# Paired dilated heads, weights of a later stage split and stored ahead, convolution taps in small groups

## The chip, the cores and the metric

The kernel runs on one core of one Trainium2 chip. The metric is the device time of one execution in microseconds. Three runs of the kernel before took 2578.41, 2578.83 and 2579.85 us, so its median is 2578.83 us.

## The reference, cut to what matters

A sequence of 512 positions with 1024 channels, in float32, goes through two blocks of two layers each.

```python
# first block, each of two layers
p = rms_norm(x, norm_g[layer]) @ w_in[layer]
a = mla_attention(...) * silu(gate_a)
b = dilated_attention(dil_qkv, cos_d, sin_d) * silu(gate_b)   # 8 heads of 64, three groups
x = x + concatenate([a, b], -1) @ w_out[layer]

# dilated attention: in each group a banded softmax attention over keys at stride 1, 4 or 16,
# then the three outputs are mixed by softmax of their log-sum-exp

# second block, layer l in (0, 1)
shift, scale, gate = split(silu(c) @ ada_w[l, s] + ada_b[l, s], 3)
h = rmsnorm(x) * (1 + scale) + shift
# l = 0: a gated recurrence (hgrn) and an rwkv mixer
# l = 1: the mixer in question
p = h @ cd_w_in                                    # 1024 x 1536
y_c = real(fftn(p[:, :512], over positions and each 128 channels))
y_d = silu(layernorm(dwconv31(val * sigmoid(gate_))))   # val, gate_ = split(p[:, 512:], 2)
x = x + gate * (concatenate([y_c, y_d], -1) @ cd_w_out)
# after each mixer, the feed forward
u, v = split(h @ w_up, 2)                          # 1024 x 5632
x = x + gate * ((silu(dwconv3(u)) * v) @ w_down)   # 2816 x 1024
```

## The kernel before

Channels lie on the 128 partitions and the 512 positions on the free axis, so x is 8 tiles of 128x512. A float32 product is made of three passes of the reduced format f32r: each operand is split into a high part and a remainder, and TensorE adds high by high, high by low and low by high (`mm3`, L130 to L132). A gemm (`gemm`) makes one 128x512 output tile from a slab of weights of 128x1024 floats (512 KB): SyncE loads the slab into `wraw`, ScalarE copies it to `whi` (L75), VectorE subtracts to `wlo` (L76), and TensorE runs 24 matmuls. The tiles `wraw`, `whi` and `wlo` have three buffers each, so a slab can be loaded three gemms ahead.

The order on each engine is not that of the code: a scheduler lays the instructions of all stages into one program for each engine. Every engine then takes its own instructions strictly in that order, SyncE its DMAs too: one that waits holds up all behind it.

Stages that matter here, by their place in the trace:

- Dilated attention, 267 to 497 us in the first layer and 820 to 1013 us in the second. `operands(p)` makes queries and keys of two heads, with rotary factors (L590 to L602; the multiply of L591 is GpSimd's). `attention(p)` handles two heads e = 0, 1, one after the other: scores `sc` (L620 to L623), maximum and exponential (L627 to L632), factors `fa` by which the three groups are weighted (L649 to L657), a multiply of the probabilities by them (L663, VectorE), transposes on TensorE into `tp` (L669, L671), copies to `pt` (L674 to L678, ScalarE), and products with the values into `po` (L683, L688). A head fills 64 of the 128 rows of `po`. There are four calls in a layer. Gemms of the next p stand in between.
- First feed forward, about 1626 to 1996 us: two halves, each of 22 gemms up and 8 gemms down. In the first half 48 slabs of modulation weights (`adaw`, 512 KB each, two buffers) are loaded for later layers and multiplied on VectorE (L719). Padded tiles `padt` are cleared at both edges by GpSimd (L750) and filled by ScalarE (L751).
- The mixer of the second block's layer 1, `m3`, 1996 to 2190 us: `conformer_in`, `fourier`, `conformer_conv` with 31 taps for each of four tiles (L1447, L1449 on VectorE; 23 taps of the last tile on TensorE through diagonal matrices `cdg` that GpSimd builds, L1439), `conformer_norm`, and `out_proj` twice. Its 24 slabs (12 of `cd_w_in`, 4 of the Fourier matrix `dft_s`, 8 of `cd_w_out`, the last as 16 halves) go the usual way through `wraw`.

Of the kernel before, what the change touches and what calls it, by code (L numbers as in the profile page):

```python
# [12 lines left out]
ALU = mybir.AluOpType  # L13
# [11 lines left out]
class Ctx:  # L25
# [165 lines left out]
    def out_proj_steps(self, pool, W, k0, mix, xcol, gate=None, done=None, norm=None, parts=None):  # L191
# [9 lines left out]
        late = 0 if norm is None else norm.late if n == 8 else 3  # L201
        for o in range(KD - late):
            xc = xcol(o)
            ps = self.gemm(W[:, o, k0:k0 + n], mh, ml, n)
            self.add_x(xc, ps, gate, o)
            if done is not None:
                done(o, xc)
            if norm is not None:
                norm.tile(o)
            yield  # L210
        if norm is not None and not late:
            norm.finish()
        if late:
            last = range(KD - late, KD)
            ws = [self.wslab(W[:, o, k0:k0 + n], [128, n, 128]) for o in last]
# [18 lines left out]
def at(x, k):  # L234

    return x[k] if isinstance(x, list) else x[:, k, :]

# [178 lines left out]
def block1_mixers(c, l, nm, mixf, side, w0, fill):  # L416
# [4 lines left out]
    if True:  # L421
# [114 lines left out]
        with ExitStack() as e2:  # L536
# [42 lines left out]
            def operands(p):  # L579
# [5 lines left out]
                for gi in range(3):  # L585
                    for j in range(2):
# [4 lines left out]
                        nc.gpsimd.tensor_tensor(sh, sh, roped[:, 1, :], op=ALU.mult)  # L591
# [15 lines left out]
            def attention(p):  # L607
                q0, k0, k0l, qk12 = qk.pop(p)
                po = c.pz.tile([128, S], F32, name="po", tag="pz")
                for e in range(2):  # L610
                    eb = slice(64 * e, 64 * e + 64)
                    hcol = slice(128 * p + 64 * e, 128 * p + 64 * e + 64)
                    st = dp.tile([128, 2, 2, 4], F32, name="st", tag="st", bufs=2)
                    nm = dp.tile([128, 2, 4], F32, name="nm", tag="nm", bufs=2)
                    pp = dp.tile([128, 4, S], F32, name="pp", tag="pp", bufs=2)
                    for i in range(4):
                        w0 = (0, 64, 192, 256)[i]
                        sc = c.px.tile([128, S], F32, name="sc", tag="px")
                        tq = slice(128 * i, 128 * i + 128)
                        nc.tensor.matmul(sc[:, 0:256], lhsT=q0[:, e, tq], rhs=k0[:, e, w0:w0 + 256], start=True, stop=False)  # L620
                        nc.tensor.matmul(sc[:, 0:256], lhsT=q0[eb, e, tq], rhs=k0l[eb, w0:w0 + 256], start=False, stop=True)
                        for gi in range(2):
                            nc.tensor.matmul(sc[:, 256 + 128 * gi:384 + 128 * gi], lhsT=qk12[eb, 0, gi, tq],  # L623
                                             rhs=qk12[eb, 1, gi, tq], start=True, stop=True)
                        for z in range(2):
                            w = slice(256 * z, 256 * z + 256)
                            nc.vector.tensor_tensor_reduce(pp[:, i, w], in0=sc[:, w], in1=dmask[:, 4 * z or i, :], scale=1.0, scalar=3 * NEG,  # L627
                                                           op0=ALU.add, op1=ALU.max, accum_out=st[:, 0, z, i:i + 1])
                        nc.vector.tensor_scalar(nm[:, :, i], st[:, 0, :, i], -0.125, None, op0=ALU.mult)  # L629
                        for z in range(2):  # L630
                            pz = pp[:, i, 256 * z:256 * z + 256]
                            nc.scalar.activation(pz, pz, AF.Exp, bias=nm[:, z, i:i + 1], scale=0.125,  # L632
                                                 accum_out=st[:, 1, z, i:i + 1])

                    ex = dp.tile([128, 2, 2, 128], F32, name="ex", tag="ex", bufs=2)
                    bc = lambda t: t.rearrange("p (z o n) -> p z o n", z=1, o=1).to_broadcast([128, 2, 4, 32])
                    nc.vector.tensor_tensor(ex[:, 0].rearrange("p z (i n) -> p z i n", i=4),
                                            st[:, :, 0, :].rearrange("p z (i o) -> p z i o", o=1).to_broadcast([128, 2, 4, 32]),
                                            bc(sel[:, 0:32]), op=ALU.mult)
                    nc.vector.tensor_tensor(ex[:, 1].rearrange("p z (n r) -> p z r n", r=4),  # L640
                                            st[:, :, 1, :].rearrange("p z (i o) -> p z i o", o=1).to_broadcast([128, 2, 4, 32]),
# [7 lines left out]
                    nc.vector.tensor_tensor(M, st[:, 0], ot[:, 0], op=ALU.max)  # L649
                    nc.vector.tensor_tensor(e1, st[:, 0], M, op=ALU.subtract)  # L650
                    nc.vector.tensor_tensor(e2_, ot[:, 0], M, op=ALU.subtract)
                    nc.scalar.activation(fa[:, 1:3], fa[:, 1:3], AF.Exp, scale=0.125)
                    nc.vector.tensor_tensor(f, e1, st[:, 1], op=ALU.mult)
# [3 lines left out]
                    nc.vector.tensor_tensor(f, f, e1, op=ALU.mult)  # L657

                    pts = []
                    for i in range(4):  # L660
                        for z in range(2):
                            pz = pp[:, i, 256 * z:256 * z + 256]
                            nc.vector.tensor_scalar(pz, pz, f[:, z, i:i + 1], None, op0=ALU.mult)  # L663

                        blocks = (((0, 0, 64, 0), (64, 0, 128, 1)), ((0, 0, 128, 1), (128, 0, 128, 2)),
                                  ((0, 0, 128, 2), (128, 0, 128, 3)), ((192, 64, 64, 0), (64, 0, 128, 3)))[i]
                        tp = c.py.tile([128, 4, 128], F32, name="tp", tag="py")
                        for j, (o, r0, n, vt) in enumerate(blocks):
                            nc.tensor.transpose(tp[0:n, j, :], pp[:, i, o:o + n], c.ident)  # L669
                        for j in range(2):  # L670
                            nc.tensor.transpose(tp[:, 2 + j, :], pp[:, i, 256 + 128 * j:384 + 128 * j], c.ident)  # L671
                        pt = dp.tile([128, 4, 128], F32, name="pt", tag="pt", bufs=4)
                        if i in (1, 2):
                            nc.scalar.activation(pt, tp, AF.Copy)  # L674
                        else:
                            r0 = blocks[0][1]
                            nc.scalar.activation(pt[r0:r0 + 64, 0, :], tp[0:64, 0, :], AF.Copy)
                            nc.scalar.activation(pt[:, 1:4, :], tp[:, 1:4, :], AF.Copy)  # L678
                        pts.append((pt, blocks))
                    for i in range(4):  # L680
                        pt, blocks = pts[i]
                        for j, (o, r0, n, vt) in enumerate(blocks):
                            nc.tensor.matmul(po[eb, 128 * i:128 * i + 128], lhsT=v0[r0:r0 + n, vt, hcol],  # L683
                                             rhs=pt[r0:r0 + n, j, :], start=i == 0 and j == 0, stop=False)
                    for i in range(4):
                        pt, _ = pts[i]
                        for j in range(2):
                            nc.tensor.matmul(po[eb, i::4], lhsT=v12[:, j, i, hcol], rhs=pt[:, 2 + j, :],  # L688
# [1353 lines left out]
```

## Time and profile before

| | |
|---|---|
| median of three runs | 2578.83 us |
| the profiled execution, device time | 2578.49 us |
| its span in the trace | 2576.7 us |
| mean granted TensorE clock | 0.976 of full speed |
| TensorE busy | 2488.2 us, 97% of the span |
| VectorE busy | 1643.1 us, 64% |
| ScalarE busy | 1074.9 us, 42% |
| GpSimd busy | 220.6 us, 9% |

The busy time of TensorE counts a matmul as running while its columns stream, and matmuls overlap by their pipelines, so intervals are read from start to start in the timeline. All DMAs of the program go through SyncE's queue (and two small queues for instructions). The share of the DMA engines is a mean over 16 engines.

### The profile page before, as it was taken

The page shows a single profiled execution, that of the slowest core. Times are in us where ns is not written, and L with a number is a line of the kernel's source. Part 1 is how long each engine was busy: PE and PEld are TensorE (multiplying, and loading weights), DVE is VectorE, ACT ScalarE, POOL GpSimd, SP SyncE. Part 2 cuts the span into 40 slices and gives each one's busy share as a digit, 9 for nine tenths or more (in the row PEclk, how much of TensorE's full clock was granted, in tenths as well). Part 3 has the DMA queues.
Part 4 walks back from the last instruction along what each step waited for, and adds up shares of the span by engine and source line. Part 5 has one row for each costly group of instructions (what it writes and reads, how often), then busy time and mean ns, then how long its engine had stood idle before and what let it go on. Part 6 is the DMA issues. An engine that isn't in the chain of part 4 may idle for free. (4 is left out here: it accounts for less than half of the span.)

```text
span 2576.7 us, 38952 instructions
## 1 busy us (share of the span) xinstructions
PE 2488.2 (97%) x15261; PEld 1999.1 (78%) x15261; DVE 1643.1 (64%) x3261; ACT 1074.9 (42%) x1947; POOL 220.6 (9%) x303
## 2 busy tenths in 40 slices
PE   8999999999999999999999888999999989999998
PEld 6769777787697777877677777878888767888887
DVE  5767666647677666576576575786444797543544
ACT  5653333526534335555434652532333424432331
POOL 0000111000001110211000130200000210100000
PEclk9999999999999999999999978999999989999999
DMA  4137121331271213321211422586333403233322
GB/s 150 45 127 241 54 58 56 109 111 40 93 278 58 58 58 95 105 74 51 88 48 55 143 81 82 190 269 209 101 88 122 149 1 97 80 88 103 96 83 81
DMA packets 92023, 265.09 MB, mean 103 GB/s; under 512 B 14528, under 2 KB 27072, under 8 KB 90944
## 3 DMA queue, kind: packets, MB, share of 16 engines
q1 hardware_dynamic: 91840, 262.61, 32.5%
q8 instruction: 120, 1.97, 0.3%
q14 instruction: 63, 0.52, 0.1%
HBM read 246.06 MB, written 16.52 MB: 102 GB/s over the span
## 5 line engine op out<-in xcount | busy, mean ns | idle before, releaser
L75 ACT ACTIVATE whi<-wraw 128x1024 fp32r<-128x1024 f32 (+3 forms) x370 | 348.5, 943 | 774.6 <-PE pg L131 563.7
L130 PE MATMUL pg<-hh,whi 128*128 128x512 f32 x1560 | 629.3, 403 | 7.9 <-ACT whi L124 6.6
L131 PE MATMUL pg<-hl,whi 128*128 128x512 f32 x1560 | 630.9, 404 | 0.0
L132 PE MATMUL pg<-hh,wlo 128*128 128x512 f32 x1560 | 628.0, 403 | 0.0
L76 DVE TENSOR_TENSOR wlo<-wraw,whi 128x1024 fp32r<-128x1024 f32 (+4 forms) x366 | 422.6, 1156 | 284.8 <-ACT whi L75 281.2
L130 PEld LDWEIGHTS pg<-hh,whi 128*128 128x128 f32 x1560 | 295.8, 190 | 88.0 <-ACT whi L124 6.6
L131 PEld LDWEIGHTS pg<-hl,whi 128*128 128x128 f32 x1560 | 295.8, 190 | 76.7 <-issue 8.1
L132 PEld LDWEIGHTS pg<-hh,wlo 128*128 128x128 f32 x1560 | 296.2, 190 | 71.6 <-issue 2.5
L132 PE MATMUL pg<-hidh,wlo 128*128 128x512 f32 (+1 forms) x396 | 145.5, 367 | 0.3 <-DVE wlo L76 0.3
L131 PE MATMUL pg<-hidl,whi 128*128 128x512 f32 (+1 forms) x396 | 145.6, 368 | 0.0
L130 PE MATMUL pg<-hidh,whi 128*128 128x512 f32 (+1 forms) x396 | 145.1, 366 | 0.0
L719 DVE CUSTOM_DVE_ANT_0 adaw<-adaw,sc 128x1024 f32<-128x1024 f32 x96 | 116.3, 1225 | 41.0 <-DMA adaw<-in_ada_w_dram 33.4
L591 POOL TENSOR_TENSOR shf<-shf,roped 128x512 f32<-128x512 f32 x48 | 62.0, 1292 | 532.7 <-ACT whi L75 249.2
L130 PE MATMUL pgv<-whi,hh 128*128 128x512 f32 (+1 forms) x240 | 89.7, 374 | 0.0
L132 PE MATMUL pgv<-whi,hl 128*128 128x512 f32 (+1 forms) x240 | 88.4, 368 | 0.0
L131 PE MATMUL pgv<-wlo,hh 128*128 128x512 f32 (+1 forms) x240 | 88.3, 368 | 0.0
L632 ACT ACTIVATE pp<-pp,nm 128x256 f32<-128x256 f32 x128 | 63.6, 497 | 54.9 <-DVE nm L629 54.8
L130 PEld LDWEIGHTS pg<-hidh,whi 128*128 128x128 f32 x396 | 74.3, 188 | 13.6 <-issue 0.4
L132 PEld LDWEIGHTS pg<-hidh,wlo 128*128 128x128 f32 x396 | 74.4, 188 | 13.1 <-DVE wlo L76 1.0
L131 PEld LDWEIGHTS pg<-hidl,whi 128*128 128x128 f32 x396 | 74.4, 188 | 12.7
L1529 ACT ACTIVATE fu<-fu 128x512 f32<-128x512 f32 x44 | 27.8, 631 | 112.2 <-DVE fu L745 112.2
L231 DVE SCALAR_TENSOR_TENSOR xT<-pg,mod,xT 128x512 f32<-128x512 f32 (+1 forms) x54 | 38.2, 710 | 48.5 <-PE pg L132 48.4
(512 smaller groups left out, 4486.2 us busy)
## 6 DMA issues: line engine op xcount, KB each, us to landing
adaw<-in_ada_w_dram SPq DMA_DIRECT2D x96, 512.0 KB, 4.6
wraw<-in_ffn_up_dram SPq DMA_DIRECT2D x88, 512.0 KB, 3.6
wraw<-in_w_dqk_dram SPq DMA_DIRECT2D x48, 512.0 KB, 3.6
wraw<-in_ffn_down_dram SPq DMA_DIRECT2D x32, 512.0 KB, 3.6
wraw<-in_w_dv_dram SPq DMA_DIRECT2D x24, 512.0 KB, 3.7
wraw<-in_w_gate_dram SPq DMA_DIRECT2D x16, 512.0 KB, 3.7
wraw<-in_w_out_dram SPq DMA_DIRECT2D x16, 512.0 KB, 3.7
wraw<-in_w_hg_dram SPq DMA_DIRECT2D x16, 512.0 KB, 3.7
```

The costliest lines, as they stand in the source:

```text
L75: nc.scalar.activation(hi, raw, AF.Copy)
L76: (eng or nc.vector).tensor_tensor(lo, raw, hi.bitcast(F32), op=ALU.subtract)
L130: mm(out, lhsT=ah, rhs=bh, start=first, stop=False)
L131: mm(out, lhsT=ah, rhs=bl, start=False, stop=False)
L132: mm(out, lhsT=al, rhs=bh, start=False, stop=last)
L231: self.nc.vector.scalar_tensor_tensor(x, in0=ps, scalar=gate[:, o:o + 1], in1=x, op0=ALU.mult, op1=ALU.add)
L591: nc.gpsimd.tensor_tensor(sh, sh, roped[:, 1, :], op=ALU.mult)
L632: nc.scalar.activation(pz, pz, AF.Exp, bias=nm[:, z, i:i + 1], scale=0.125, accum_out=st[:, 1, z, i:i + 1])
L719: nc.vector.tensor_tensor_reduce(w, in0=w, in1=sc, scale=1.0, scalar=0.0, op0=ALU.mult, op1=ALU.add, accum_out=mod[:, j:j + 1])
L1529: nc.scalar.activation(u, u, AF.Silu)
```

## The change

**Dilated heads.** The two heads of a call go together: the score matmuls, the copies and the `po` matmuls are written in turns of e = 0 and e = 1, so that neighbours use different halves of TensorE's rows or columns. VectorE's multiply L663 is gone. In its place ScalarE builds, for every head and block of 128 queries, two diagonal matrices `dg` of 128x128 with the factors (L705 of the changed kernel), and the transposes become fp32 matmuls of the probabilities against `dg` (L709, L711). `pt` reuses the memory of `pp`, with a clearing by GpSimd for the edge blocks. The rotary multiply L591 moves from GpSimd to VectorE.

**Weights ahead.** A class `Parts` takes each of the 24 slabs of `m3`: inside the first feed forward it loads the slab (`praw`, two buffers, SyncE), splits it (`phi` on ScalarE, `plo` on VectorE, two buffers each) and writes both parts to DRAM, 512 KB each, by DMAs of GpSimd's queue. In `m3` a gemm loads the two parts straight into `whi` and `wlo` and splits nothing.

**Taps.** `conformer_conv` becomes a class `Conv`, whose `taps(n)` is called between the gemms of `conformer_in` and `fourier`; the diagonal matrices, TensorE's taps and what is left follow in `rest`, after the first step of the first half of `out_proj`.

```diff
     def wslab(self, src, shape, raw=None, eng=None, out=None):
+        if isinstance(src, Parts):
+            hl = out or [self.w.tile(shape, F32R, name=t, tag=t) for t in ("whi", "wlo")]
+            for t, z in zip(hl, src.parts):
+                nc.sync.dma_start(t.bitcast(F32), z)
+            return hl
...
+class Parts:
+    def __init__(self, c, src, name):
+        self.src = src.rearrange("p k n -> p (k n)")
+        self.parts = [c.dram.tile([128, 1024], F32, name=f"{name}{z}") for z in "hl"]
+    def make(self, c, pool):
+        raw = pool.tile([128, 1024], F32, name="praw", tag="praw", bufs=2)
+        c.nc.sync.dma_start(raw, self.src)
+        hl = [pool.tile([128, 1024], F32R, name=t, tag=t, bufs=2) for t in ("phi", "plo")]
+        c.split(*hl, raw)
+        for z, t in zip(self.parts, hl):
+            c.nc.gpsimd.dma_start(z, t.bitcast(F32))
...
-                        nc.gpsimd.tensor_tensor(sh, sh, roped[:, 1, :], op=ALU.mult)
+                        nc.vector.tensor_tensor(sh, sh, roped[:, 1, :], op=ALU.mult)
...
-                            nc.vector.tensor_scalar(pz, pz, f[:, z, i:i + 1], None, op0=ALU.mult)
+                            nc.scalar.activation(dg[:, z], c.ident, AF.Copy, scale=fs[e][:, z, i:i + 1])
...
-                            nc.tensor.transpose(tp[0:n, j, :], pp[:, i, o:o + n], c.ident)
+                            mm(tp[0:n, j, :], lhsT=pp[e, i][:, o:o + n], rhs=dg[:, 0], start=True, stop=True)
...
+                for i in range(4):
+                    for j in range(2):
+                        for e, eb, hcol in es:
+                            pt, blocks = pts[e, i]
+                            nc.tensor.matmul(po[eb, 128 * i:128 * i + 128], lhsT=v0[:, blocks[j][3], hcol], rhs=pt[:, j, :],
+                                             start=i == 0 and j == 0, stop=False)
...
+    def taps(self, n):
+        nc, cw, acc = self.c.nc, self.cw, self.acc
+        while n and self.todo and self.todo[0][0] < len(self.hds):
+            j, t = self.todo.pop(0)
...
             ps = c.gemm(I["ffn_up"][l][:, 2 * j], hh, hl)
             p = padded(c, fp, ps)
+            if ahead is not None:
+                ahead()
...
         for o in range(KD - late):
             c.side()
+            if ahead is not None and not hf:
+                ahead()
...
-                cv = conformer_in(c, dp, hh, hl)
-                fourier(c, dp, hh, hl, mixf)
+                cv = Conv(c, dp)
+                conformer_in(c, dp, hh, hl, cv)
+                fourier(c, dp, hh, hl, mixf, cv)
                 x = load_x(Norm, *spec)
-                acc = conformer_conv(c, dp, hp, cv)
-                conformer_norm(c, dp, acc, mixf)
-                c.out_proj(mp, W, 0, [mixf[:, k] for k in range(4)], x, gate)
+                half = c.out_proj_steps(mp, W, 0, [mixf[:, k] for k in range(4)], x, gate)
+                next(half)
+                cv.rest(dp, hp)
+                conformer_norm(c, dp, cv.acc, mixf)
+                for _ in half:
+                    pass
...
+                todo = [c.parts["in"][k] for k in (8, 4, 9, 5, 10, 6, 11, 7, 0, 1, 2, 3)] + c.parts["dft"] + c.parts["out"]
+                ahead = lambda: todo and todo.pop(0).make(c, fp)
```

Where the scheduler puts things shows in the programs of the engines. A row there gives the line, the instruction, its output and inputs with tile numbers, and the shape.

On TensorE, at the end of the first layer's first attention call, the kernel before runs the `po` matmuls of one head in a row:

```order
L671 MATMUL tp_2311<-c_ident_81,pp_2222 128x128 x2
L683 MATMUL po_2219<-pt_2288,v0_1512 64x128
L683 MATMUL po_2219<-pt_2298,v0_1512 64x128 x2
L683 MATMUL po_2219<-pt_2307,v0_1512 64x128 x2
L683 MATMUL po_2219<-pt_2316,v0_1512 64x128 x2
L688 MATMUL po_2219<-pt_2288,v12_1513 64x128 x2
L688 MATMUL po_2219<-pt_2298,v12_1513 64x128 x2
L688 MATMUL po_2219<-pt_2307,v12_1513 64x128 x2
L688 MATMUL po_2219<-pt_2316,v12_1513 64x128 x2
L646 MATMUL ot_2381<-sel_1510,ex_2378 128x4 x4
```

In the changed kernel, at the same place, inputs of head 0 (`pp_2226`, `pp_2268`) and head 1 (`pp_2227`, `pp_2269`) alternate:

```order
L711 MATMUL tp_2416<-dg_2413,pp_2269 128x128 x2
L725 MATMUL po_2219<-pp_2269,v0_1512 64x128
L725 MATMUL po_2219<-pp_2268,v0_1512 64x128
L725 MATMUL po_2219<-pp_2269,v0_1512 64x128
L725 MATMUL po_2219<-pp_2268,v0_1512 64x128
L725 MATMUL po_2219<-pp_2269,v0_1512 64x128
L725 MATMUL po_2219<-pp_2268,v0_1512 64x128
L135 MATMUL pg_2551<-hh_103,whi_2547 128x512
L725 MATMUL po_2219<-pp_2269,v0_1512 64x128
L730 MATMUL po_2219<-pp_2226,v12_1513 64x128
L730 MATMUL po_2219<-pp_2227,v12_1513 64x128
```

The number of `po` matmuls is the same; neighbours now belong to different heads and so to different halves of the output rows. In all 256 of them, counted over the whole program, 116 pairs of neighbours of different heads can be formed, which leaves 140 places in the queue.

On SyncE, in the middle of the 22 up gemms of the first feed forward, the kernel before loads two `adaw` slabs for one `wraw`:

```order
L718 DMA adaw_15300<-in_ada_w_dram 128x1024
L718 DMA adaw_15339<-in_ada_w_dram 128x1024
L67 DMA wraw_15333<-in_ffn_up_dram 128x1024
L718 DMA adaw_15381<-in_ada_w_dram 128x1024
L718 DMA adaw_15420<-in_ada_w_dram 128x1024
L67 DMA wraw_15375<-in_ffn_up_dram 128x1024
L718 DMA adaw_15462<-in_ada_w_dram 128x1024
L718 DMA adaw_15501<-in_ada_w_dram 128x1024
L67 DMA wraw_15414<-in_ffn_up_dram 128x1024
L718 DMA adaw_15543<-in_ada_w_dram 128x1024
```

In the changed kernel loads of `praw` stand among them:

```order
L254 DMA praw_15425<-in_cd_w_in_dram 128x1024
L67 DMA wraw_15388<-in_ffn_up_dram 128x1024
L760 DMA adaw_15355<-in_ada_w_dram 128x1024
L67 DMA wraw_15438<-in_ffn_up_dram 128x1024
L760 DMA adaw_15394<-in_ada_w_dram 128x1024
L254 DMA praw_15514<-in_cd_w_in_dram 128x1024
L760 DMA adaw_15444<-in_ada_w_dram 128x1024
L67 DMA wraw_15477<-in_ffn_up_dram 128x1024
L760 DMA adaw_15483<-in_ada_w_dram 128x1024
L254 DMA praw_15603<-in_cd_w_in_dram 128x1024
L67 DMA wraw_15527<-in_ffn_up_dram 128x1024
L760 DMA adaw_15533<-in_ada_w_dram 128x1024
```

For each pair of up gemms there are now about two `adaw`, one or two `praw` and two `wraw`, and the missing `adaw` loads stand later, among the loads of the down gemms. GpSimd's queue issues two stores for each `praw`.

On ScalarE, at the start of the down gemms, the kernel before has the splits of the down weights (a slab of 128x1024 and one of 128x384 for each gemm) after the last `hidh`; `whi_15793` is the second down gemm's, `whi_15893` the fourth's:

```order
L75 ACTIVATE whi_15793<-wraw_15791 128x1024
L124 ACTIVATE hidh_15734<-fu_15694 128x512
L75 ACTIVATE whi_15799<-wraw_15797 128x384
L75 ACTIVATE whi_15843<-wraw_15841 128x1024
L75 ACTIVATE whi_15849<-wraw_15847 128x384
L75 ACTIVATE whi_15893<-wraw_15891 128x1024
L75 ACTIVATE whi_15899<-wraw_15897 128x384
```

In the changed kernel `whi_15993` is the second down gemm's and `whi_16109` the fourth's, and the last splits of the 24 slabs, `phi`, stand between:

```order
L129 ACTIVATE phi_16518<-praw_16516 128x1024
L129 ACTIVATE hidh_15918<-fu_15878 128x512
L129 ACTIVATE phi_16607<-praw_16605 128x1024
L80 ACTIVATE whi_15999<-wraw_15997 128x384
L80 ACTIVATE whi_16051<-wraw_16049 128x1024
L129 ACTIVATE phi_16696<-praw_16694 128x1024
L80 ACTIVATE whi_16057<-wraw_16055 128x384
L129 ACTIVATE phi_16785<-praw_16783 128x1024
L80 ACTIVATE whi_16109<-wraw_16107 128x1024
```

The 24th `phi` (`phi_16785`) now stands directly ahead of the fourth down gemm's `whi_16109`; all 24 slabs are split before the fourth of the 8 down gemms.

## Rows read from the trace of the kernel before

**Rows 1.** page of the profile, busy time of each engine, and the chain that ended last

```profile
PE 2488.2 (97%) x15261; PEld 1999.1 (78%) x15261; DVE 1643.1 (64%) x3261; ACT 1074.9 (42%) x1947; POOL 220.6 (9%) x303
...
PE 34%; DVE 4%; DMA 3%; issue 2%; POOL 1%; ACT 1%; DVEq 0%; POOLq 0%; ACTq 0%
```

**Rows 2.** stages: stretch, length, busy (x count) of PE PEld DVE ACT POOL, PEclk, DMA share, GB/s

```profile
267.00:497.00 230.00, 227.87 (x1186) 176.15 (x1185) 153.65 (x430) 101.91 (x244) 24.53 (x19) 0.99 0.20 60
820.00:1013.00 193.00, 190.93 (x1002) 147.43 (x1000) 124.89 (x345) 80.26 (x189) 22.56 (x19) 0.99 0.19 54
1626.30:1748.40 122.10, 121.19 (x563) 98.37 (x562) 102.23 (x156) 47.99 (x71) 7.71 (x20) 1.00 0.74 234
1748.40:1809.50 61.10, 60.74 (x264) 49.11 (x263) 34.54 (x52) 14.38 (x18) 0.10 (x1) 1.00 0.63 196
1996.00:2190.00 194.00, 175.18 (x887) 145.83 (x885) 158.00 (x246) 73.39 (x129) 28.12 (x22) 0.94 0.27 84
```

**Rows 3.** timeline of PE in a dilated attention call: start us, us

```profile
289.49 0.38 PE L669 MATMUL tp<-c_ident,pp 128*64 128x128 f32 x2
289.70 0.38 PE L671 MATMUL tp<-c_ident,pp 128*128 128x128 f32 x2
...
292.11 2.03 PE L683 MATMUL po<-pt,v 128*64 128x128 f32 x14
293.98 1.91 PE L688 MATMUL po<-pt,v 128*64 128x128 f32 x16
295.82 1.05 PE L646 MATMUL ot<-sel,ex 128*128 128x4 f32 x8
```

**Rows 4.** timeline of PE in MLA attention

```profile
108.11 3.65 PE L532 MATMUL po<-ptm,vm 128*64 128x512 f32 x14
111.69 0.98 PE L527 MATMUL tp<-c_ident,pe 128*128 128x128 f32 x7
```

**Rows 5.** groups by line, 267 to 497 us: busy us, mean ns, idle before and its releaser

```profile
L76 DVE TENSOR_TENSOR wlo<-wraw,whi 128x1024 fp32r<-128x1024 f32 x23 | 37.9, 1649 | 0.2 <-ACT whi L75 0.2
...
L591 POOL TENSOR_TENSOR shf<-shf,roped 128x512 f32<-128x512 f32 x19 | 24.5, 1291 | 160.5 <-DVE shf L590 79.4 <-DVE nm L629 45.7 <-ACT whi L75 35.4
...
L592 DVE TENSOR_TENSOR xr<-pg,roped 128x512 f32<-128x512 f32 x19 | 12.9, 678 | 0.1
...
L663 DVE TENSOR_SCALAR pp<-pp,fa 128x256 f32<-128x256 f32 x64 | 17.5, 344 | 0.1
...
L632 ACT ACTIVATE pp<-pp,nm 128x256 f32<-128x256 f32 x64 | 31.8, 498 | 27.6 <-DVE nm L629 27.5
...
L674 ACT ACTIVATE pt<-tp 128x512 f32<-128x512 f32 x16 | 9.5, 593 | 5.6 <-PE tp L671 5.6
...
L669 PE MATMUL tp<-c_ident,pp 128*64 128x128 f32 (+1 forms) x64 | 12.3, 274 | 1.8 <-DVE pp L663 1.8
```

**Rows 6.** DMA, 1640 to 1780 us: queue with MB and share of 16 engines; issues

```profile
q1 hardware_dynamic: 10389, 36.15, 81.0%
...
adaw<-in_ada_w_dram SPq DMA_DIRECT2D x45, 512.0 KB, 4.4
```

**Rows 7.** DMA, 215 to 235 us, GB/s in 40 slices of 0.5 us

```profile
GB/s 426 426 434 418 418 401 418 361 246 360 360 369 418 385 295 344 410 328 336 401 442 393 377 385 393 426 401 410 410 369 156 41 33 16 156 164 369 311 49 0
```

**Rows 8.** timeline of SP, ACT and PE, first feed forward

```profile
1637.42 0.33 SPq L718 DMA_DIRECT2D adaw<-in_ada_w_dram  x1
...
1764.06 1.06 ACT L75 ACTIVATE whi<-wraw 128x1024 fp32r<-128x1024 f32 x1 [2.13 <-DMA wraw<-in_ffn_down_dram]
...
1771.28 0.40 PE L131 MATMUL pg<-hidl,whi 128*128 128x512 f32 x1
```

**Rows 9.** timeline of POOL, DVE and PE, last Fourier group

```profile
2095.41 6.25 POOL L1439 TENSOR_TENSOR cdg<-c_ident,cwh 128x2944 fp32r<-128x2944 f32 x1 [80.27 <-PE pg L132]
...
2102.16 5.59 DVE L125 TENSOR_TENSOR ful<-fu,fuh 128x512 fp32r<-128x512 f32 x1
...
2107.80 0.80 PE L132 MATMUL psf<-CH,ful 128*128 128x256 f32 x2 [9.79 <-DVE ful L125]
```

More of the change, by code (lines that the diff above doesn't have):

```diff
@@ L609, in attention @@
                 po = c.pz.tile([128, S], F32, name="po", tag="pz")
[L610 to L623, printed above, removed]
+                es = [(e, slice(64 * e, 64 * e + 64), slice(128 * p + 64 * e, 128 * p + 64 * e + 64)) for e in range(2)]
@@ new lines, in conformer_in, with __init__, rest @@
+        cv.hds.append(hd)
+        cv.taps(6)
+class Conv:
+    def __init__(self, c, dp):
+        self.c = c
+        self.hds = []
+        self.cw = c.load(dp, "dconv_w", [128, 4, 31])
+        self.cb = c.load(dp, "dconv_b", [128, 4])
+        self.acc = dp.tile([128, 4, S], F32, name="cacc")
+        self.todo = [(j, t) for j in range(4) for t in range(CT if j == 3 else 31)]
+    def taps(self, n):
+        nc, cw, acc = self.c.nc, self.cw, self.acc
+        while n and self.todo and self.todo[0][0] < len(self.hds):
+            j, t = self.todo.pop(0)
+            o, x, w = acc[:, j, :], self.hds[j][:, t:t + 512], cw[:, j, t:t + 1]
+            if t == 0:
+                nc.vector.tensor_scalar(o, x, w, self.cb[:, j:j + 1], op0=ALU.mult, op1=ALU.add)
+            else:
+                nc.vector.scalar_tensor_tensor(o, in0=x, scalar=w, in1=o, op0=ALU.mult, op1=ALU.add)
+            n -= 1
+    def rest(self, dp, hp):
+        c, nc, cw = self.c, self.c.nc, self.cw
+        n = 31 - CT
+        dh, dl = (hp.tile([128, 32, 128], F32R, name="cdg", tag=t, bufs=1) for t in ("hh", "hl"))
+        flat = lambda t: t[:, 26:].rearrange("p a b -> p (a b)")[:, 0:S + 30]
+        hh, hl = flat(dh), flat(dl)
+        c.split(hh, hl, self.hds[3])
+        wh = dp.tile([128, 31], F32R, name="cwh")
+        wl = dp.tile([128, 31], F32R, name="cwl")
+        c.split(wh, wl, cw[:, 3])
+        for d, w in ((dh, wh), (dl, wl)):
+            nc.gpsimd.tensor_tensor(d[:, 0:n], c.ident.rearrange("p (o q) -> p o q", o=1).to_broadcast([128, n, 128]),
+                                    w[:, CT:].bitcast(F32).rearrange("p (t o) -> p t o", o=1).to_broadcast([128, n, 128]), op=ALU.mult)
+        pc = c.pz.tile([128, S], F32, name="pcv", tag="pz")
+        for t in range(n):
+            x = slice(CT + t, CT + t + S)
+            c.mm3(pc, dh[:, t], dl[:, t], hh[:, x], hl[:, x], t == 0, t == n - 1)
+        self.taps(99)
+        nc.vector.tensor_tensor(self.acc[:, 3], self.acc[:, 3], pc, op=ALU.add)
@@ L1483, in fourier @@
     for z in range(4):
-        raw = c.w.tile([128, 2, S], F32, name="wraw", tag="wraw")
-        nc.sync.dma_start(raw, I["dft_s"][:, 2 * z:2 * z + 2])
-        c.split(DH[:, 2 * z:2 * z + 2], DL[:, 2 * z:2 * z + 2], raw)
+        c.wslab(c.parts["dft"][z].cut(S), None, out=[t[:, 2 * z:2 * z + 2] for t in (DH, DL)])
     craw = c.load(dp, "dft_c", [128, 256])
@@ L1491, in fourier @@
     for g in range(4):
-        ps = c.gemm(I["cd_w_in"][:, g], hh, hl)
+        ps = c.gemm(c.parts["in"][g].cut(128), hh, hl)
+        cv.taps(6)
         uf = c.t2("fu")
```

138 lines of the change are left out of this document (69 added, 69 removed).

## Prediction

> **What bounds the kernel now.** The page is read first: TensorE is busy 97% of the span, and the chain that ended last is mostly its own [rows 1]. Work taken off another engine pays only where TensorE waits for it; an engine or a queue that becomes late costs its whole delay. The stretches come next [rows 2]. In the dilated stages TensorE idles 230.00 − 227.87 = 2.1 us and 2.1 us of the four calls each, and VectorE has 67% and 65%. In the first feed forward TensorE idles under 1 us in 122, while VectorE has 84% and the DMA engines already have 74% of their time, for 234 GB/s. In `m3` TensorE idles 194.0 − 175.2 = 18.8 us and its granted clock is 0.94. So the dilated stages can gain only by TensorE's own work, `m3` by a wait, and the feed forward has nothing to give and a DMA load that is high before anything is added. That stage I expect to decide.
>
> **Dilated heads: −8 us.** TensorE first. Two transposes take 289.70 − 289.49 = 0.21 us, 0.105 each; 16 passes of `po` take 295.82 − 293.98 = 1.84 us, 0.115 each [rows 3]. An fp32 matmul runs as two passes (a `po` line of 8 instructions is x16 there), a transpose as one. Both layers have 256 transposes, so 256 × 0.105 = 26.9 us become 512 × 0.115 = 58.9 us; by the cheaper row's 0.105 they become 53.8. That is +27 to +32 us, and I take +29.
>
> Against it, `po`: 256 instructions, 512 passes, 58.9 us. In MLA attention heads already alternate: 14 passes of 512 columns took 111.69 − 108.11 = 3.58 us, 0.256 each [rows 4], while a pass of 128 columns at 0.105 makes 0.42 for 512. Neighbours of different column halves thus run in 0.256 / 0.42 = 0.61 of the time, the changes of shape included. With 140 places in place of 256, halving gives 58.9 × 116 / 256 = −26.7 us, and the ratio 0.61 gives −23; I take −25. Scores pair only for the first block of four, which no row here prices: 0 to −4 us, taken −2. A change of array shape costs about 293.98 − 292.11 − 14 × 0.115 = 0.26 us [rows 3]; by the order of instructions there are some 30 round trips fewer (80 to 64 in rows, 88 to 74 in columns), −8 us. TensorE: 29 − 25 − 2 − 8 = −6.
>
> VectorE loses 128 multiplies of 0.344 us (44 us) and takes 48 rotary ones at 0.678 (33 us, after L592); its splits, 1.649 us in this stretch, may get shorter when GpSimd's 1.291 us multiplies no longer run beside them [rows 5]. Behind VectorE TensorE waits 1.8 us at L669 in a layer, so 2 × 1.8 us goes at most; I take −2. Both layers need 128 `dg`. The nearest row is a ScalarE pass with a pointer over 256 columns, 0.498 us; a `dg` has 128, so half and all of it, 0.25 and 0.50, bound it, and I take 0.39, since a part of an instruction does not shrink with its columns: 50 us of ScalarE, which has about 56% idle in these stretches [rows 2, 5]. It hides behind gemms except inside a call, where a tile needs two `dg` and a copy, 2 × 0.39 + 0.59 = 1.37 us, beside TensorE's 8 × 0.115 + 0.25 = 1.17: 8 tiles may cost 8 × 0.2 = 1.6 us a call, 13 in eight calls. Copies overlap at their ends, so I take 0. The part is −6 − 2 = −8, from −20 to +12.
>
> **Weights ahead: +26 us.** Each of the 24 slabs adds a load and two stores of 512 KB, 0.524 MB, in all 37.7 MB. Up to now 36.15 MB filled 81% of the 16 engines in 140 us [rows 6], so they would be full at 36.15 / 140 / 0.81 = 319 GB/s. When more transfers are outstanding they move more: the slices from 215 to 230 us, filled with the same two kinds of load, average 385 GB/s, and slices stand between 246 and 442 [rows 7].
>
> The deadline lies in ScalarE's order: the 24th `phi` stands ahead of the fourth down gemm's split. That split ran at 1764.06 and the gemm began near 1771.3 [rows 8], so the `phi` must end by about 1770. Before it SyncE must have passed everything up to the 24th `praw`. The third `adaw` load started at 1637.42 [rows 8], when VectorE had freed the first buffer; it stands at the same place after the change, two `praw` earlier. From it to the 24th `praw` I count in the changed order 30 `adaw`, 22 `praw` and 20 `wraw` of 512 KB, and 4 of 192 KB. The 24th `phi` needs the buffer of the 22nd, whose store is the 42nd in GpSimd's queue. That makes 114 × 0.524 + 4 × 0.197 = 60.6 MB. At 385 GB/s it takes 157 us and ends at 1794.8; with 1.06 us for the `phi` [rows 8] the split is free at 1795.9, 26 us after its deadline. TensorE stands still for that in pieces, as each load before it is late too. What is left for the later down gemms (about 10 MB, 25 us) fits in their time, and the second half of the feed forward, with `wraw` alone, does not give the delay back, since TensorE is the bound there. By the best slices of 442 GB/s the term is +5 us, by 319 GB/s +58; I take +26 by the mean. VectorE's 24 added splits, below 24 × 1.649 = 40 us, fill most of what it has free there (16% of 122 us, and more behind it), which goes the same way.
>
> What GpSimd's DMA issues cost no row shows, since the kernel before has none; below by 0 (hidden), above by its heaviest row, a 1.291 us multiply, for 48 issues 62 us on an engine with 9% busy. What is queued behind them are the clearings of `padt`, two tiles ahead, so 0.
>
> The Trainium skill ("DMA: Bandwidth & Descriptors", section "Issuing engines are not separate DMA queues") says that DMAs from any engine run on the same 16 engines and interleave, so another queue saves issue time only; by that the stores count in full, as I count them. Its section "Where 436 GB/s comes from" gives 435 GB/s as the fabric's ceiling and about 358 as what HBM gives one core: an estimate by these would be +8 or +38 us in place of +26. The slices of 418 to 442 [rows 7] go past the lower figure for short times.
>
> **`m3`: −3 us.** Without the splits, and with the taps in groups, VectorE has 24 splits less. TensorE gains only where it waits. The longest wait is 9.79 us for `ful` [rows 9]: VectorE's two subtractions (a 128x512 pass takes it 0.678 [rows 5]) hold until GpSimd's two builds of `cdg` end (2095.41 + 6.25 = 2101.7 for the first; `ful` ended at 2107.75). After the change `ful` comes first in VectorE's order and the split of `cdg` second, but the builds start at the same event, the last read of `hh`: `ful` waits for the first build, about 4.2 us, and `fal`, behind the other split, for the second, about 4. So 8.3 in place of 9.8, −1.5; half-speed time after a wait and fewer late splits at the stage's start give the rest. The new loads (two of 512 KB for each gemm, into buffers freed three gemms before) have two gemms' time, 11 us, against 4.4 us to landing [rows 6], and hide. If the clock's loss goes too, 0.06 × 194 = 11 us: range −12 to +4. The taps stood among the gemms before, by the scheduler, so the class itself moves little.
>
> **Sum.** −8 + 26 − 3 = +15, and 2578.49 + 15 = 2593.5 for the profiled execution, which lies 0.3 us below the median: 2594. A measurement of this kernel can tell about 0.2%, 5.2 us, from no change.
>
> **Rivals.**
> - *The stores cost nothing beside the loads* (opposite directions), so faster. Then 72 × 0.524 + 0.8 = 38.5 MB take 100 us and end at 1737, before the deadline: −8 − 3, 2568. For it: no row shows a stage with as many stores as loads. Against it: the engines were at 81% with loads alone. It decides from about 450 GB/s, at which 60.6 MB end at 1772.
> - *The changes cancel*: DMA at about 430 GB/s, or attention at the good end of its range: 2574 to 2584.
> - *Attention loses too*: the `dg` builds hold up the transposes, +13 us on top: 2607. For it the 1.37 against 1.17 us a tile; against it the gemms in between.
> - *The DMA engines stay at 319 GB/s*: +58 − 11, 2625. Against it, the fuller queue of rows 7.
> - *Nothing*: the taps were interleaved, the diagonals eat the pairing, the transfers hide: about 2577.
>
> **How the numbers follow.** Forecast, slower by 6 to 32 us: 0.42 (own range 2584 to 2610). With attention losing too: 0.07, DMA slow: 0.06. Stores free or nearly so: 0.30. Cancelling, or nothing: 0.15. So faster 0.30, same 0.15, slower 0.55. The range reaches to the free stores below with a good attention part (2562) and above to a rate of about 350 GB/s (2578.5 − 11 + 42 = 2610) with part of the ScalarE waits: 2562 to 2620.
>
> **What would show it.** Right: between 1640 and 1790 us the DMA share is near 1.0 at about 400 GB/s, ScalarE waits for DMA at `phi`, TensorE idles some 25 us behind `whi`, and the second half of the feed forward starts that much late, less what the dilated stages gained. In attention the `po` matmuls start in pairs and the transposes come as x256. In `m3` a wait of about 4 us stays at `ful`. Wrong: TensorE without gaps in the feed forward (the stores then cost no time or the rate passes 450), or gaps at L709 behind `dg`.

## The result, and the profile after

The changed kernel took 2605.57 us (median of four runs, 2602.23 to 2606.72) against 2578.62 us for the kernel before in the same comparison: ratio 1.0103, with a 95% interval of 1.0089 to 1.0117. It is slower by 27 us; 2594 was forecast.

Page of the changed kernel: busy time, DMA share and rate in 40 slices, and the two queues that move data (packets, MB, share of 16 engines).

```profile
PE 2490.2 (96%) x15517; PEld 2000.2 (77%) x15517; DVE 1612.0 (62%) x3174; ACT 1110.6 (43%) x2067; POOL 186.8 (7%) x334
...
DMA  4146221331362214312212333999533713223322
GB/s 149 44 138 229 61 61 50 123 96 45 134 233 59 64 49 124 97 45 70 73 43 81 126 101 103 358 387 353 162 91 119 286 41 116 88 85 99 100 82 80
...
q1 hardware_dynamic: 99904, 287.78, 34.0%
q0 software_dynamic: 6912, 25.17, 2.4%
```

TensorE is busy for as long as before, 2490.2 us [rows 1], in a span that is 26.7 us longer. Three slices of 65 us, from 1627 to 1822 us, have a DMA share of 9 tenths and more; q0 is GpSimd's queue, with 25.17 MB that did not exist before.

Stretches of the changed kernel, columns as in [rows 2]: the first layer's dilated stage, the up gemms and the down gemms of the first feed forward's first half, and `m3`.

```profile
267.00:482.00 215.00, 214.46 (x1274) 167.19 (x1272) 129.00 (x372) 113.59 (x295) 3.18 (x16) 1.00 0.19 55
1617.00:1764.50 147.50, 128.89 (x564) 102.05 (x563) 112.00 (x155) 65.48 (x90) 28.24 (x59) 0.95 0.92 349
1764.50:1838.40 73.90, 65.15 (x264) 49.62 (x263) 48.27 (x71) 18.88 (x23) 5.41 (x11) 0.98 0.91 331
2024.50:2218.00 193.50, 176.62 (x899) 148.54 (x898) 137.16 (x224) 51.83 (x104) 25.12 (x21) 0.94 0.42 147
```

The up and down gemms took 147.5 and 73.9 us, 122.1 and 61.1 before [rows 2]; TensorE was idle for 18.6 and 8.8 of them, 27.4 together (1.3 before), and its granted clock was 0.95 and 0.98, where it had been 1.00. The DMA share is 0.92 at 349 GB/s, the quiet first 10 us included, and 0.91 at 331.

The start times of marked matmuls put the change in its place. All are read from the timeline of TensorE.

| | before | changed | moved by |
|---|---|---|---|
| last `po`, end of the second dilated stage | 1012.3 | 1003.2 | −9.1 |
| last `phs`, shortly before the first feed forward | 1576.1 | 1567.3 | −8.8 |
| first matmul on `hidh` (down gemms) | 1748.4 | 1764.5 | +16.1 |
| last matmul of the first feed forward | 1995.9 | 2024.5 | +28.6 |
| first matmul on `hidh` in the second feed forward | 2318.6 | 2345.0 | +26.4 |
| end of the span | 2576.7 | 2603.4 | +26.7 |

So the dilated heads gained 9, the first feed forward lost 37, and `m3` gained 2. Of the 37, TensorE's idle time makes 26; time at the lower of TensorE's two clock levels (1.2 GHz, called half-speed time below) makes about 9 more, an estimate from the two granted clocks: 0.05 × 147.5 + 0.02 × 73.9.

Waits of the changed kernel from 1620 to 1845 us: engine, what waited, for whom; us in total, times, longest.

```profile
ACT phi L129 <- DMA praw<-in_cd_w_in_dram: 31.6, 9, 7.7
DVE adaw L761 <- DMA adaw<-in_ada_w_dram: 28.0, 22, 4.0
ACT phi L129 <- DMA praw<-in_cd_w_out_dram: 24.0, 7, 5.9
...
ACT phi L129 <- DMA praw<-in_dft_s_dram: 16.0, 3, 6.5
PE pg L135 <- DVE fu L1588: 14.8, 5, 4.1
```

The chain is to be read from the bottom up. Loads land late; ScalarE stands 72 us at 19 of the 24 splits, VectorE 28 us at `adaw`; each then comes late to what is queued behind, on VectorE the multiply L1588 that frees a result of TensorE. TensorE itself never waits for a DMA: its longest sum names VectorE. No wait at a split names a store, so it is not the buffers `phi` and `plo`, held until they are written out, that make ScalarE late.

### The profile page after: what moved, and what is told of

Read it like the earlier page. It is cut to its first block, busy times and chain, and to the rows that moved or that the text cites. A ratio compares the mean times of both kernels' runs of the same rounds, so it can differ in the third digit from the quotient of the medians.

```text
span 2603.4 us, 39715 instructions
## 1 busy us (share of the span) xinstructions
PE 2490.2 (96%) x15517; PEld 2000.2 (77%) x15517; DVE 1612.0 (62%) x3174; ACT 1110.6 (43%) x2067; POOL 186.8 (7%) x334
## 3 DMA queue, kind: packets, MB, share of 16 engines
q0 software_dynamic: 6912, 25.17, 2.4%
## 5 line engine op out<-in xcount | busy, mean ns | idle before, releaser
L135 PE MATMUL pg<-hh,whi 128*128 128x512 f32 x1560 | 633.0, 406 | 26.1 <-DVE fu L1588 14.8
L80 ACT ACTIVATE whi<-wraw 128x1024 fp32r<-128x1024 f32 (+3 forms) x342 | 325.0, 953 | 699.0 <-PE pg L136 513.6
L81 DVE TENSOR_TENSOR wlo<-wraw,whi 128x1024 fp32r<-128x1024 f32 (+4 forms) x339 | 371.6, 1097 | 273.6 <-ACT whi L80 270.1
L1485 DVE SCALAR_TENSOR_TENSOR cacc<-chd,l_dconv_w,cacc 128x512 f32<-128x512 f32 x97 | 72.2, 798 | 0.5
```

What stands on the lines that cost most here:

```text
L135: mm(out, lhsT=ah, rhs=bh, start=first, stop=False)
L1485: nc.vector.scalar_tensor_tensor(o, in0=x, scalar=w, in1=o, op0=ALU.mult, op1=ALU.add)
```

## The experiments

Medians of runs on one chip for each group, beside the kernel before: 2578.42 us for the first four kernels, 2577.43 for the next four, 2577.74 for the last three.

**1. The heads alone** (`e_att`): the kernel before with the three pieces of the diff in `operands` and `attention`.

> Only the dilated heads are changed; weights and taps are as before. Theory (the delay of the changed kernel is the DMA load of the first feed forward, the heads gain about 9 us): 2578.6 - 9 = 2569.6, between 2566 and 2573. Rival (the diagonal builds on ScalarE cost what the pairing gains): 2577 to 2592.

Measured 2573.25 us, ratio 0.9982 (0.9971 to 0.9994), a gain of 5. In its trace the two layers, from the V gemms to the last `po`, take 332.2 us each, before 338.1 and 336.6: 10.4 for both, about what was forecast. What is missing was lost at other places, 1.0 us between the two layers and 2.4 us between the last `po` and the next stage. The rival falls, by little: its range begins at 2577, and the interval ends there.

**2. The slabs not ahead** (`e_noparts`): heads and taps as changed, weights as before. From experiment 1 it differs by the class `Conv` and the new order of `m3` alone.

```diff
-        ps = c.gemm(c.parts["in"][8 + j].cut(128), hh, hl)
+        ps = c.gemm(I["cd_w_in"][:, 8 + j], hh, hl)
...
-                todo = [c.parts["in"][k] for k in (8, 4, 9, 5, 10, 6, 11, 7, 0, 1, 2, 3)] + c.parts["dft"] + c.parts["out"]
-                ahead = lambda: todo and todo.pop(0).make(c, fp)
```

> The changed kernel with its 24 slabs loaded and split in the mixer again, nothing made ahead; heads and Conv stay. Theory: the feed forward runs as before, so 2578.6 - 9 and 0 to 3 for the taps' new order, 2566 to 2572. Rival (the taps or the heads' end cost the time): 2590 or more.

Measured 2587.66 us, ratio 1.0033 (1.0019 to 1.0046): the theory was wrong here. From the last `phs` to the end of the feed forward it needs 418.7 us, before 419.8, so the delay of the changed kernel is gone with the slabs. But `m3` became 13 us longer (335.8 us from the last matmul of one feed forward to the first `hidh` of the next; 322.7 before, 324.4 in `e_att`, 320.5 in the changed kernel). Its waits from 1991 to 2190 us:

```profile
ACT DH L129 <- DMA wraw<-in_dft_s_dram: 15.4, 3, 8.3
...
PE pg L135 <- ACT whi L80: 9.3, 2, 7.7
```

The splits of the Fourier matrix wait for their loads on ScalarE, and the weights of the next gemm stand behind them; TensorE waits 9.3 us. In `e_att` the same splits of ScalarE waited 3.1 us, and no wait of TensorE named `whi`. So in the changed order of `m3` the slabs made ahead are worth some 15 us, and the new order costs 11 without them; the prediction, with −3 for both together, did not see these apart.

**3. The stores left out** (`e_nostore`).

```diff
-        for z, t in zip(self.parts, hl):
-            c.nc.gpsimd.dma_start(z, t.bitcast(F32))
+        if self.first:
+            for z, t in zip(self.parts, hl):
+                c.nc.gpsimd.dma_start(z, t.bitcast(F32))
```

> The changed kernel in which only the first slab's two parts are stored, and every gemm of the mixer loads these two; so 46 of 48 stores of 512 KB are left out and the result is not the reference's, while all loads and all 24 splits stay in their places. Theory (bytes): 60.6 - 22 = 38.5 MB up to the 24th slab take about 102 us at 380 GB/s, before the deadline, so the delay goes nearly whole: 2566 to 2575. Rival (splits and their place in the queues of ScalarE and VectorE): the delay stays at 25 us or more of 37, 2592 to 2606.

Measured 2571.91 us, ratio 0.9977 (0.9964 to 0.9990). Up gemms and down gemms of the first half:

```profile
1628.00:1745.00 117.00, 114.81 (x509) 91.60 (x509) 108.35 (x147) 59.95 (x74) 5.00 (x16) 1.00 0.85 293
1745.00:1808.00 63.00, 61.47 (x266) 49.43 (x266) 48.62 (x71) 18.09 (x23) 0.10 (x1) 1.00 0.85 283
```

All loads and splits are there, VectorE's share of the up gemms is even higher than in the changed kernel, and TensorE idles 2.2 and 1.5 us in place of 18.6 and 8.8, at a granted clock of 1.00. Of the 37 us some 5 are left (424.5 us from `phs` to the end of the feed forward, 419.8 before, 457.2 changed). So the stores' bytes make the delay, not the splits or their place in the queues.

**4. The stores on another queue** (`e_actstore`): `c.nc.scalar.dma_start` in place of `c.nc.gpsimd.dma_start` in `make`.

> The changed kernel with its 48 stores issued by ScalarE's queue in place of GpSimd's. Theory (bytes on the same 16 engines): the delay stays, 2598 to 2615. Rival (GpSimd's queue makes the stores slow or holds up its other work): 2585 or less.

Measured 2616.79 us, ratio 1.0162 (1.0134 to 1.0190). The same two stretches:

```profile
1628.00:1774.00 146.00, 121.53 (x505) 95.57 (x505) 113.17 (x155) 58.16 (x72) 2.10 (x12) 0.92 0.96 367
1774.00:1847.00 73.00, 64.76 (x263) 50.22 (x262) 46.76 (x69) 19.22 (x23) 0.10 (x1) 0.95 0.90 318
```

The share and rate are about those of the changed kernel, whose row for the same first stretch is

```profile
1628.00:1774.00 146.00, 126.60 (x524) 99.15 (x523) 114.56 (x156) 59.87 (x76) 22.91 (x52) 0.95 1.00 380
```

and the delay is a few us more (464.1 us from `phs` to the end of the feed forward), which put the time just above the theory's range. GpSimd's queue is not the cause.

**5. The slabs spread out** (`e_tied`, then `e_tied2`). A 128x1 write by VectorE into the slab's buffer, with a value of the last finished tile, makes the load wait for that tile.

```diff
+        c.nc.vector.tensor_scalar(raw[:, 0:1], after, 1.0, None, op0=ALU.mult)
         c.nc.sync.dma_start(raw, self.src)
...
+            if ahead is not None and hf:
+                for _ in range(1 + jj % 2):
+                    ahead(u[:, 0:1])
```

> The changed kernel with each slab's load tied to the progress of the feed forward by a 128x1 VectorE write of its buffer, so that 4 slabs are made in the down gemms of the first half and 20 in the second half. The same bytes and splits, at most about 300 GB/s. Theory: no delay, 2578.6 - 9 - 2 and 0 to 4 for the splits, 2565 to 2573. Rival (stores by GpSimd's queue or the splits themselves cost TensorE time wherever they stand): 2590 or more.

Measured 2589.47 us, ratio 1.0044 (1.0029 to 1.0059): slower than the kernel before, and at the edge of the rival's range. The first half was nearly as before (236.3 us from the last `phs` to the end of its down gemms; 233.5 before, 271.1 in the changed kernel), but the second lost 20 us. Its waits from 1800 to 2010 us:

```profile
ACT phi L129 <- DMA praw<-in_cd_w_in_dram: 37.5, 8, 7.4
ACT phi L129 <- DMA praw<-in_cd_w_out_dram: 36.3, 7, 6.9
...
PE pg L135 <- ACT whi L80: 6.4, 4, 2.3
```

The load now starts when its turn comes, but ScalarE has the split directly behind it in its program and stands at it for 74 us, with the weights of the next gemm behind. The rate was 267 GB/s from 1800 to 2010 us, below the 380 of the changed kernel, so this is not a lack of bandwidth. `e_tied2` holds the split back by one step in the same manner, gives `praw` a third buffer for it, and places a few slabs otherwise in the down gemms:

```diff
+    def make(self, c, pool, after):
+        raw = self.raw
...
+        c.nc.vector.tensor_scalar(hl[0][:, 0:1], after, 1.0, None, op0=ALU.mult)
         c.split(*hl, raw)
```

> As e_tied, but the split of a slab waits for the next step of the feed forward, so that its load has a step of 5 to 11 us to land before ScalarE comes to it, with three raw buffers. Theory (in e_tied ScalarE stood at a split whose load was on its way, with the weights of the next gemm queued behind): the 17 us that e_tied lost in the second half go, 2568 to 2576. Rival (24 splits and 48 stores cost TensorE time by their mere presence): 2583 or more.

Measured 2569.98 us, ratio 0.9967 (0.9954 to 0.9980), faster than both kernels. Second half of its feed forward:

```profile
1804.00:1928.00 124.00, 124.00 (x533) 99.77 (x532) 81.21 (x124) 55.47 (x70) 16.87 (x39) 1.00 0.84 295
1928.00:1990.00 62.00, 61.92 (x342) 53.66 (x341) 34.09 (x62) 23.59 (x35) 7.33 (x19) 1.00 0.77 268
```

The same bytes at about the same rate, and TensorE busy without a gap; no wait at `phi` is left among the longest. The third buffer was not tried by itself. `m3` takes 318.5 us, 6 less than in `e_att`; for the whole kernel the gain over `e_att` is some 3 us, with intervals that overlap.

**6. The taps where they were** (`e_tapsback`): `e_tied2` without the calls `cv.taps(6)` and `cv.taps(7)`, and with `rest` ahead of `out_proj`. `taps(99)` then stops two short of 101, so two taps of the last tile are left out, 1.5 us of VectorE.

> e_tied2 with the taps written after the Fourier part again and the first half of out_proj after the convolution, as in the kernel before; the slabs stay split ahead. Theory (the scheduler puts the taps among the gemms wherever they are written): as e_tied2 within 4 us, 2566 to 2574. Rival (the groups of taps gain or cost by themselves): 2578 or more, or 2562 or less.

Measured 2570.94 us, ratio 0.9976 (0.9962 to 0.9990), and `m3` 319.2 us. Where the slabs are split ahead, the grouping of the taps does nothing, as the prediction said; where they are not, the new order cost 11 us (experiment 2), which it did not say.

**7. Pairs with transposes** (`e_pairtrans`, then `e_pairmem`): on `e_att`, the diagonals undone.

```diff
-                            nc.scalar.activation(dg[:, z], c.ident, AF.Copy, scale=fs[e][:, z, i:i + 1])
+                            pz = pp[e, i][:, 256 * z:256 * z + 256]
+                            nc.vector.tensor_scalar(pz, pz, fs[e][:, z, i:i + 1], None, op0=ALU.mult)
...
-                            mm(tp[0:n, j, :], lhsT=pp[e, i][:, o:o + n], rhs=dg[:, 0], start=True, stop=True)
+                            nc.tensor.transpose(tp[0:n, j, :], pp[e, i][:, o:o + n], c.ident)
```

> e_att with the heads still paired, but the diagonals undone: VectorE's multiply and the one-pass transposes are back. Theory (the prediction's term: 256 transposes became 512 passes, +27 to +32 us of TensorE): 2573 - 29 and 0 to 8 for VectorE's waits, 2543 to 2553. Rival (the diagonal matmuls cost about what transposes cost, or VectorE's multiply holds up TensorE as much): 2566 to 2578.

Measured 2561.00 us, ratio 0.9936 (0.9921 to 0.9952), 12 below `e_att`, between the two theories. Timelines of GpSimd, VectorE and TensorE at the first call:

```profile
287.99 3.00 POOL L689 MEMSET pp<- 64x128 f32 x1 [137.26 <-DVE pp L677]
291.88 0.20 POOL L689 MEMSET pp<- 64x128 f32 x1 [0.89 <-PE tp L681]
...
287.36 3.50 DVE L677 TENSOR_SCALAR pp<-pp,fa 128x256 f32<-128x256 f32 x13
...
291.05 0.43 PE L697 MATMUL po<-pp,v 128*64 128x128 f32 x2 [2.58 <-POOL pp L689]
```

GpSimd's clearing of an edge block, 0.20 us at other times, takes 3.00 us and ends when VectorE's row of 13 multiplies does, and `po` waits for it: 9.2 us a layer. TensorE also ran at half speed for some us after such a wait (matmuls of 0.63 us in place of 0.38 at 293 us). With the clearing on VectorE (`nc.vector.memset`):

> e_pairtrans with the clearing of the edge blocks on VectorE in place of GpSimd. Theory (GpSimd's clearing was held for 3.0 us behind a row of 13 VectorE multiplies, and TensorE waited 9.2 us a layer for it): these waits go, 2561 - 18 and 0 to 6 less for half-speed time, 2537 to 2545; the diagonals then cost 28 to 36 us against transposes, as predicted. Rival (VectorE is late by itself, and TensorE waits for it in place of GpSimd): 2552 or more.

Measured 2536.27 us, ratio 0.9837 (0.9810 to 0.9864). A layer takes 311.0 us, 332.2 with the diagonals: these cost 2 × 21.2 = 42 us, more than the 28 to 36 expected. (That the clearing is on another engine does not blur this: with the diagonals GpSimd's took 0.20 us each, and no matmul waited for one.)

**8. Small builds** (`e_pieces`): on `e_att`, `cdg` built in 46 instructions of 128x128 in place of two of 128x2944.

> e_att with GpSimd's two builds of the diagonal matrices for the convolution cut into 46 of 128x128. Theory (VectorE's operations with two SBUF inputs are held as long as one GpSimd instruction runs, so the 9.8 us wait at ful was the length of a build): the wait shrinks to 1 us or so and the half-speed time behind it goes, 2573 - 8 to - 14, 2559 to 2566. Rival (VectorE is held for the whole of the builds whatever their length, or 46 instructions take much longer than two): 2571 or more.

Measured 2567.49 us, ratio 0.9963 (0.9949 to 0.9976), between the theory and the rival: 5.8 below `e_att`, or 4.9 by the two ratios, whose intervals just overlap. The traces are clearer: `m3` takes 318.3 us against 324.4. Its waits of TensorE from 1992 to 2190 us, and the builds (busy us, mean ns, idle before):

```profile
PE psb L161 <- DVE rsy L148: 2.7, 1, 2.7
PE pcv L130 <- POOL cdg L1454: 2.1, 7, 0.3
...
L1454 POOL TENSOR_TENSOR cdg<-c_ident,cwh 128x128 fp32r<-128x128 f32 x23 | 17.0, 738 | 80.1 <-PE pg L132 80.1
L1454 POOL TENSOR_TENSOR cdg<-c_ident,cwl 128x128 fp32r<-128x128 f32 x23 | 16.8, 730 | 0.0
```

The wait at `ful`, 9.8 us in `e_att`, is down to 0.4. The builds take 34 us in place of 12, and TensorE waits 2.1 us for them in all.

**9. All that helped** (`e_all`): `e_tied2`, transposes and VectorE's clearing, small builds.

> e_tied2 with the transposes and VectorE's multiply and clearing of e_pairmem, and the pieces of e_pieces. If the gains add: 2570 - 30 for the transposes without GpSimd's wait, - 6 for the pieces, 2528 to 2540. Rival (the pieces fill the same wait as the parts, or VectorE becomes late with the multiplies): 2546 or more.

Measured 2522.57 us, ratio 0.9781 (0.9756 to 0.9805): 55 us below the kernel before. The second half of its feed forward, and `m3`:

```profile
1760.00:1950.00 190.00, 190.00 (x856) 155.33 (x854) 116.40 (x175) 80.05 (x101) 25.32 (x55) 1.00 0.84 294
1950.00:2140.00 190.00, 182.37 (x967) 153.85 (x967) 132.24 (x237) 53.45 (x107) 34.92 (x73) 0.97 0.45 156
```

By their ratios the three gains make 51 us, so they add within the noise. `m3` takes 308.0 us, where the two changes to it, 6 us each, would give 312.

## Why the prediction was right, point by point

**The bound.** That the first feed forward would decide, with its DMA load, held: share 1.00, ScalarE at `phi` behind loads, TensorE waiting in pieces. One sign did not come as told: TensorE was to idle behind `whi`, and of its waits only 1.6 us name `whi`, 14.8 the multiply of VectorE. Three rows of the changed kernel's timeline, the third `adaw` load, the 24th `praw` load and the 24th `phi`, and the stretch between them:

```profile
1628.17 0.33 SPq L760 DMA_DIRECT2D adaw<-in_ada_w_dram  x1
...
1784.08 0.44 SPq L254 DMA_DIRECT2D praw<-in_cd_w_out_dram  x1
...
1791.03 1.06 ACT L129 ACTIVATE phi<-praw 128x1024 fp32r<-128x1024 f32 x1 [5.78 <-DMA praw<-in_cd_w_out_dram]
...
1628.17:1791.03 162.86, 142.71 (x589) 110.92 (x587) 124.34 (x168) 63.60 (x81) 25.55 (x57) 0.96 1.00 382
1760.00:1780.00 20.00, 18.26 (x75) 14.02 (x74) 11.85 (x18) 7.43 (x10) 2.78 (x7) 0.98 1.03 417
1792.00:1838.40 46.40, 40.81 (x164) 31.61 (x165) 31.39 (x47) 9.91 (x13) 1.06 (x2) 0.96 0.84 288
```

The prediction's 60.6 MB in 1791.03 − 1628.17 = 162.9 us are 372 GB/s, where 385 was taken from [rows 7]; all that the stretch moved, a few transfers for other work with it, is 382. The stage began 9.2 us earlier than before, by the heads' gain, so the deadline moved to 1760.8, and the `phi` ended at 1792.1: 31 us late, forecast 26. Experiments 3 and 4 show that it is the bytes. The rival of free stores falls with them: the 22 MB of stores in the sum took the time that their bytes take at the same rate.

**What was mis-sized.** The step "what is left for the later down gemms fits in their time" failed by some 7 us: the down gemms ended 38 us late, not 31. It held bytes against time, and the DMA engines were indeed no longer full (0.84 at 288 GB/s from 1792 us on). But VectorE went on standing at `adaw` loads, and TensorE behind VectorE's `wlo` and `xT`, at a granted clock of 0.96. Waits from 1792 to 1840 us:

```profile
DVE adaw L761 <- DMA adaw<-in_ada_w_dram: 14.9, 12, 4.0
...
PE pg L137 <- DVE wlo L81: 3.3, 5, 1.2
PE pg L135 <- DVE xT L237: 3.1, 1, 3.1
```

The stage thus cost 37 us where the sum had 26: 5 by the rate (162.9 us in place of 157) and the rest behind the deadline. That two terms beside it were wrong inside and came out near, as follows, is luck.

The Trainium skill ("DMA: Bandwidth & Descriptors", section "Issuing engines are not separate DMA queues") has all DMAs on the same 16 engines whatever queue issues them; the trace agrees, 380 GB/s with GpSimd's queue and 367 with ScalarE's from 1628 to 1774 us. Its section "Where 436 GB/s comes from" gives about 358 GB/s for HBM to one core, by which the prediction's estimate for this term was +38 us. 31 were measured at the deadline, and the stage moved 382 GB/s over 163 us and 417 from 1760 to 1780 us, loads and stores together, so the runs do not show this figure as a ceiling.

**Dilated heads.** −8 was forecast and −9 measured, but by luck, out of two terms that were both too small. The changed kernel's timeline of TensorE at one call:

```profile
293.08 0.85 PE L709 MATMUL tp<-dg,pp 128*64 128x128 f32 x4
293.77 0.61 PE L711 MATMUL tp<-dg,pp 128*128 128x128 f32 x4
294.21 0.61 PE L709 MATMUL tp<-dg,pp 128*128 128x128 f32 x4
294.66 0.61 PE L711 MATMUL tp<-dg,pp 128*128 128x128 f32 x4
...
303.23 0.32 PE L725 MATMUL po<-pp,v 128*64 128x128 f32 x1
303.24 0.32 PE L730 MATMUL po<-pp,v 128*64 128x128 f32 x1
303.39 0.27 PE L725 MATMUL po<-pp,v 128*64 128x128 f32 x1
303.40 2.01 PE L730 MATMUL po<-pp,v 128*64 128x128 f32 x31
305.34 0.50 PE L136 MATMUL pg<-hl,whi 128*128 128x512 f32 x1
```

Four passes take 0.44 or 0.45 us, but the first four of an edge tile, one of whose outputs has 64 rows, 0.69. An inner tile thus takes 0.89, an edge tile 1.13, and a tile of four transposes takes 0.43 (289.49 to 289.92 in the kernel before): 32 × (0.89 + 1.13) − 64 × 0.43 = +37 us by these rows, and 42 by experiment 7, forecast +29. The pairs pay more than forecast as well: 34 passes of `po` take 305.34 − 303.23 = 2.11 us, 0.062 each, 0.54 of the 0.115 when alone. What all else in the heads' change gains together (pairs, fewer changes of shape, the rotary multiply on VectorE, waits) is then 10.4 + 42.3 = 53 us from the kernel before to `e_pairmem`, forecast 35 and 2 of waits; how it divides among them was not tested. ScalarE's `dg` took 0.391 us, forecast 0.39, and no wait of TensorE's matmuls named it.

**`m3`.** −3 forecast, −2 measured, and again by luck. `ful` waited 9.24 us in place of the 4.2 of the prediction:

```profile
2123.29 5.91 POOL L1499 TENSOR_TENSOR cdg<-c_ident,cwh 128x2944 fp32r<-128x2944 f32 x1 [80.74 <-PE pg L137]
2129.16 5.55 POOL L1499 TENSOR_TENSOR cdg<-c_ident,cwl 128x2944 fp32r<-128x2944 f32 x1
...
2124.14 5.60 DVE L1485 SCALAR_TENSOR_TENSOR cacc<-chd,l_dconv_w,cacc 128x512 f32<-128x512 f32 x1
2129.67 5.59 DVE L130 TENSOR_TENSOR ful<-fu,fuh 128x512 fp32r<-128x512 f32 x1
...
2135.31 0.79 PE L137 MATMUL psf<-CH,ful 128*128 128x256 f32 x2 [9.24 <-DVE ful L130]
```

The step "`ful` comes first in VectorE's order" left out the tap between: it started 0.85 us after the first build, was held to its end (5.60 us), and `ful` was then held for the second. And the new order of the stage, which the prediction had at next to nothing, costs 11 us by itself; the slabs made ahead paid for it (experiment 2). In `e_tapsback`, with the old order (and two taps short), `m3` is 5 us shorter than in `e_att`.

## What to carry to other kernels

Work that is moved into a stage "with idle engines" has to be summed in bytes up to a deadline, with the stores counted as loads: here 60.6 MB had to pass before one split, and the sum at the rate of the best sustained rows gave the delay to within a third. A load that was spread out helped only when its consumer stood later in its own engine's program; before, the wait had moved into that engine's queue. A change of several parts is worth taking apart: heads that lost 42 us to one part and gained 53 by the others, an order that cost 11 us without the slabs, and two GpSimd instructions that held VectorE, were found only so.

## What the runs showed of the hardware

- A GpSimd clearing of 64x128, which reads nothing, took 3.00 us while VectorE ran 13 single-input multiplies from SBUF to SBUF in a row, and 0.20 us otherwise. The other way round, a VectorE operation with two SBUF inputs was held 5.6 us by one GpSimd build, a tap as well as a subtraction. Cut into 46 pieces of some 0.8 us each, the builds let such operations pass one by one, 0.88 us each.
- Stretches with the same instructions differed by their half-speed time. Between the last `po` and the next V gemms 163.5 us passed before, at a granted clock of 0.98, and 165.9 in the changed kernel; 173.4 in `e_pairmem`, at 0.93 (0.90 over the last 82 us), and 173.6 in `e_all`, also at 0.93. This gave back part of what the dilated stages gained, and why the clock stays low longer in some programs was not settled.
